# The recurrence's step of a two-layer decoder trunk, with the gate's matmuls set at other places between the groups of small products

## The chip, the cores and the metric

The kernel runs on one core of a Trainium2 chip. The metric is device time in microseconds of one execution, the median of several runs. The core has five engines with a queue each: TensorE (PE, matmuls; PEld is its loading of weights), VectorE (DVE), ScalarE (ACT), GpSimd (POOL) and SyncE (SP), which here only issues DMAs.

## The reference

Two layers over 1024 tokens of width 1024, in float32. The first (gated spatial mixing beside dilated attention) isn't touched. The second is RWKV-7 time mixing: for each of 16 heads of 64 channels a state of 64 x 64 is carried from token to token, and a SiLU gate is multiplied in before the last projection.

```python
def step(state, inp):
    r_t, w_t, k_t, v_t, kk_t, a_t = inp
    sa = jnp.einsum('bhvk,bhk->bhv', state, -kk_t)
    state = (state * w_t[:, :, None, :]
             + sa[..., None] * (kk_t * a_t)[:, :, None, :]
             + v_t[..., None] * k_t[:, :, None, :])
    y_t = jnp.einsum('bhvk,bhk->bhv', state, r_t)
    return state, y_t
...
y = (y + bonus.reshape(B, S, D)).astype(h.dtype) * jax.nn.silu(g)    # g = xg @ w_g
return y @ w_o
```

## The kernel before, in words

The recurrence is computed in 16 chunks of 64 tokens, two chunks to a pair. Within a chunk the token-by-token update is written as products of 64 x 64 blocks, one for each head, and the inverse of a triangular matrix of each head; from chunk to chunk the state S is carried. A product of 64 x 64 uses a quarter of TensorE's array, and a head's products stand in groups: 16 heads, each float32 product as two matmuls, so 32 matmuls and as many weight loads a group (64 where two groups are interleaved).

The matmuls of the gate (x @ w_g, in three float32r products for each block of weights) are independent of the recurrence. They are cut into 128 pieces of three matmuls of 128 x 128 by 128 x 512, and `g1`, `g2` in an order put one or two such pieces at that place. A block of weights for it is loaded (`gl`) and split into a high and a low part (`gx`: a copy on ScalarE, then a subtraction on VectorE, lines 105 and 106).

The order of all engines' work in this part is written out by hand, as strings of names: SCAN_START, then SCAN_STEP six times, then SCAN_END. Each name is a method; each engine executes its own instructions in the order in which the names issue them, so a name's place sets its place on each engine it uses, and on SP's queue for its DMAs. Semaphores are put in from the data's dependences. In a step (chunks c, c+1, with work ahead for c+2 to c+5) the names are:

- `U` (lines 1241 to 1254): products of the inverse X with Ws, interleaved on TensorE with `Wkeys` of the next chunk (line 1225), then two copies to UV on ScalarE.
- `st` (1268 to 1277): products of UV with the transposed keys, then VectorE adds them to the state S; `keep` (1266): GpSimd multiplies S by the decay for the chunk after.
- `Y` and `W` (1285, 1235, 1294): the output's products; those of the state with A, of the next chunk, interleaved with the output's second part; then copies of Ws and Y on ScalarE. W needs the addition of `st`, and the next U needs Ws.
- `al` (1043 to 1048): two groups of products of A with BK, to M and AK through ScalarE's copies; `mA` masks AK on GpSimd. `sM` (1055) stores M, `lM` (1099) loads it again in another layout as Nt.
- `sc` (1030, 1031): the scores' products of A and BK and their copy to MY; `mY` (1084) masks MY of an earlier pair on GpSimd.
- `dec` (1062): GpSimd multiplies BK by the decay in place; `T` (1072, 1073): TensorE transposes the decayed BK.
- `ip`, `ia`, `ie`, `ib` (1106 to 1164): the inversion on VectorE from Nt, of which `ib2`, `ib3` are two and three of the eight parts of its rows; `ic` (1171) stores the inverse (XT<-xm), `lX` (1179) loads it as X. `mx`, `ma`, `mb` (1185, 1197, 1200, 1210, 1213) complete X on VectorE, TensorE and ScalarE.
- `ld`, `uv`, `Yd`, `gl`: loads of A and BK, of v, the store of Y, the load of the gate's weights, all on SP.

TensorE's order in a step is therefore U0 al0 st0 al1 Y0 W1 sc0 U1 sc1 g st1 Y1 g W2 sc2 T0 g sc3 ma0 g2 mb0 g2 T1 g2; SP's is uv1 sM0 ld6 ic0 lM0 lX0 uv2 Yd0 ld7 gl2.

Of the kernel before, what the change touches and what calls it, by code (L numbers as in the profile page):

```python
# [56 lines left out]
SCAN_STEP = (  # L57
    "U0 al0 ib2 st0 al1 Y0 uv1 keep1 mA0 mA1 W1 sM0 sc0 ib3 ld6 U1 sc1 g1 mY0 mY1 ic0 st1 dec0 lM0 Y1 g1 W2 keep2 "
    "ip0 lX0 gx1 uv2 sc2 Yd0 T0 g1 sc3 ia0 ld7 mx0 ma0 dec1 ie0 g2 mb0 g2 T1 g2 ib3 gl2")
SCAN_END = (  # L60
# [1504 lines left out]
```

## Time and profile before

| | |
|---|---|
| median of 3 runs | 1482.53 us (1478.01 to 1484.24) |
| the profiled execution's own time | 1480.0 us |
| span of its instructions | 1478.1 us |
| mean granted clock of TensorE | 0.941 |
| busy: PE / PEld / DVE / ACT / POOL | 1308.3 / 1108.9 / 897.8 / 627.8 / 548.4 us |

The span goes from the first to the last instruction. A busy TensorE isn't one at its peak: matmuls overlap and their ends are modelled. The granted clock is the share of 2.4 GHz that the throttle let through; it has two levels, 1.2 and 2.4 GHz, so 0.941 is a mean over both. The six steps of the recurrence lie between 1089 and 1293 us of the span, the end after them.

### The profile page before, as it was taken

The page shows a single profiled execution, that of the slowest core. Times are in us where ns is not written, and L with a number is a line of the kernel's source. Part 1 is how long each engine was busy: PE and PEld are TensorE (multiplying, and loading weights), DVE is VectorE, ACT ScalarE, POOL GpSimd, SP SyncE. Part 2 cuts the span into 40 slices and gives each one's busy share as a digit, 9 for nine tenths or more (in the row PEclk, how much of TensorE's full clock was granted, in tenths as well). Part 3 has the DMA queues.
Part 4 walks back from the last instruction along what each step waited for, and adds up shares of the span by engine and source line. Part 5 has one row for each costly group of instructions (what it writes and reads, how often), then busy time and mean ns, then how long its engine had stood idle before and what let it go on. Part 6 is the DMA issues. An engine that isn't in the chain of part 4 may idle for free.

```text
span 1478.1 us, 30910 instructions
## 1 busy us (share of the span) xinstructions
PE 1308.3 (89%) x12773; PEld 1108.9 (75%) x12773; DVE 897.8 (61%) x1489; ACT 627.8 (42%) x1188; POOL 548.4 (37%) x353
## 2 busy tenths in 40 slices
PE   5899999899997999999997868998978788887877
PEld 5887788778896799978864436896767666667877
DVE  8741535663557426771599888512856677768884
ACT  4421535552454323552545554323434344454322
POOL 8750102030112612221343353203644444387751
PEclk9999999899999999999999979998978898979998
DMA  6377435350443334224177547517586666676412
GB/s 221 86 259 196 114 128 158 83 131 15 137 121 101 124 119 143 74 74 140 43 220 203 125 103 204 143 48 207 142 244 162 154 168 167 187 212 228 143 36 93
DMA packets 253275, 209.15 MB, mean 141 GB/s; under 512 B 79648, under 2 KB 215424, under 8 KB 253136
## 3 DMA queue, kind: packets, MB, share of 16 engines
q1 hardware_dynamic: 249536, 198.27, 47.1%
q10 hardware_dynamic: 3600, 8.91, 1.8%
q8 instruction: 100, 1.64, 0.5%
q14 instruction: 39, 0.32, 0.1%
HBM read 135.71 MB, written 71.43 MB: 140 GB/s over the span
## 4 chain that ended last, share of the span: by engine, by line
PE 53%; DVE 17%; DMA 9%; issue 8%; ACT 6%; POOL 4%; SPq 2%; ACTq 0%; DVEq 0%; POOLq 0%
PE pj L153 33%; PE pj L943 4%; PE pt L572 2%; PE pj L1477 2%; DMA kl<-dk 1%; DMA BK<-BK_d 1%; DMA w<-in_rw_a_dram 1%; DMA XT<-xm 1%; PE sp L562 1%; PE sp L559 1%; PE op L580 1%; DMA X<-XT 1%; ACT wh L105 1%; PE py L1285 1%; DVE xm L737 1%
## 5 line engine op out<-in xcount | busy, mean ns | idle before, releaser
L106 POOL TENSOR_TENSOR wl<-wraw,wh 128x1024 fp32r<-128x1024 f32 x38 | 93.6, 2466 | 168.6 <-ACT wh L105 157.5
L106 DVE TENSOR_TENSOR wl<-wraw,wh 128x1024 fp32r<-128x1024 f32 x46 | 70.8, 1545 | 94.5 <-ACT wh L105 51.4
L153 PE MATMUL pj<-hh,wh 128*128 128x512 f32 x320 | 127.3, 398 | 0.0
L153 PE MATMUL pj<-hh,wl 128*128 128x512 f32 x320 | 126.6, 396 | 0.0
L153 PE MATMUL pj<-hl,wh 128*128 128x512 f32 x320 | 126.6, 396 | 0.0
L105 ACT ACTIVATE wh<-wraw 128x1024 fp32r<-128x1024 f32 x84 | 88.1, 1056 | 61.9 <-DMA wraw<-in_w_in_even_dram 25.1
L153 PE MATMUL pj<-xl,wh 128*128 128x512 f32 x256 | 102.3, 400 | 2.6 <-DVE xl L740 2.6
L153 PE MATMUL pj<-xh,wh 128*128 128x512 f32 x256 | 102.2, 401 | 2.4 <-ACT ks L789 2.4
L153 PE MATMUL pj<-xh,wl 128*128 128x512 f32 x256 | 101.8, 398 | 0.2 <-POOL wl L106 0.2
L566 DVE CUSTOM_DVE_ANT_0 sc<-sp,tb 128x128 f32<-128x128 f32 (+3 forms) x64 | 48.2, 753 | 59.4 <-PE sp L562 50.8
L1477 PE MATMUL pj<-wh,yh 128*128 128x256 f32 x256 | 75.4, 294 | 5.1 <-DVE x L1481 3.9
L1477 PE MATMUL pj<-wh,yl 128*128 128x256 f32 x256 | 74.4, 291 | 4.6 <-POOL yl L106 4.5
L153 PE MATMUL pj<-wh,hh 128*128 128x256 f32 x256 | 75.1, 296 | 3.2 <-ACT hh L265 2.9
L737 DVE SCALAR_TENSOR_TENSOR xm<-hT,pr,xm 128x512 f32<-128x512 f32 x56 | 50.0, 933 | 44.0 <-ACT xm L736 43.7
L153 PE MATMUL pj<-wh,hl 128*128 128x256 f32 x256 | 75.3, 295 | 1.2 <-DVE hl L266 1.2
L153 PE MATMUL pj<-wh,yl 128*128 128x256 f32 x256 | 73.7, 288 | 1.9 <-POOL yl L624 1.9
L153 PE MATMUL pj<-wl,hh 128*128 128x256 f32 x256 | 74.6, 292 | 0.0
L153 PE MATMUL pj<-wh,yh 128*128 128x256 f32 x256 | 73.3, 286 | 0.8 <-ACT yh L623 0.8
L1477 PE MATMUL pj<-wl,yh 128*128 128x256 f32 x256 | 74.0, 289 | 0.0
L153 PE MATMUL pj<-wl,yh 128*128 128x256 f32 x256 | 72.9, 285 | 0.0
L153 PE MATMUL pj<-wh,xh 128*128 128x256 f32 x256 | 72.2, 282 | 0.6 <-ACT ks L789 0.5
L153 PE MATMUL pj<-wl,xh 128*128 128x256 f32 x256 | 72.2, 282 | 0.0
(320 smaller groups left out, 4062.3 us busy)
## 6 DMA issues: line engine op xcount, KB each, us to landing
wraw<-in_w_in_even_dram SPq DMA_DIRECT2D x28, 512.0 KB
tb<-tb SPq DMA_DIRECT2D x16, 512.0 KB
A_d<-AR SPq DMA_DIRECT2D x16, 512.0 KB
wraw<-in_rw_wg_dram SPq DMA_DIRECT2D x16, 512.0 KB
A<-A_d SPq DMA_DIRECT2D x16, 512.0 KB
BK<-BK_d SPq DMA_DIRECT2D x16, 512.0 KB
xt<-in_x_dram SPq DMA_DIRECT2D x8, 512.0 KB
dv<-vt SPq DMA_DIRECT2D x16, 256.0 KB
```

Source lines behind the costliest of these rows:

```text
L105: nc.scalar.activation(hi, raw, AF.Copy)
L106: sub.tensor_tensor(lo, raw, hi.bitcast(F32), OP.subtract)
L153: nc.tensor.matmul(ps, a(k), b(k), start=(n == 0), stop=(n == 3 * KT - 1))
L559: nc.tensor.matmul(sp[:, c0:c1], qs[:, b * P:(b + 1) * P], kh[:, c0:c1], start=True, stop=False)
L562: nc.tensor.matmul(sp[:, c0:c1], qs[:, b * P:(b + 1) * P], kl[:, c0:c1], start=False, stop=True)
L566: nc.vector.tensor_tensor_reduce(sc[:, :n], sp[:, :n], tb[:, off:off + n], 1.0, BIG, OP.add, OP.min, mn)
L572: nc.tensor.transpose(pt[:, j - j0, :], sc[:, j * P:(j + 1) * P], g.ident)
L580: nc.tensor.matmul(op[:, s0:QW], vt[:, j, :], pth[j // 4][:, j % 4, s0:QW], start=(j == 0), stop=False)
L737: nc.vector.scalar_tensor_tensor(t, hT[kk, f][:, j, 0:512], g.pr[:, i, k:k + 1], t, op0=OP.mult, op1=OP.add)
L943: nc.tensor.matmul(ps, u[:, k], v[:, k % 2], start=(k == 0 and i == 0), stop=(k == KT - 1 and i == 2))
L1285: nc.tensor.matmul(self.py[64 - 64 * e:128 - 64 * e, q], t["MY"][:, 8 * e + q], t["UV"][:, e, q], start=q == 0, stop=False)
L1477: nc.tensor.matmul(ps[:, i, :], u[:, k], v[:, k % 4], start=(k == 0 and j == 0), stop=(k == KT - 1 and j == 2))
```

## The change

The string of the step is written anew; no name is added or left out (the pieces of the gate are nine in both). On TensorE the order becomes U0 al0 g st0 Y0 g W1 al1 U1 g g st1 Y1 sc0 g W2 sc1 T0 g sc2 sc3 ma0 g2 mb0 T1 g. So al1 goes behind W1 (and with it its two copies, mA1 and sM0's data), sc0 behind Y1, sc1 behind W2, T0 ahead of sc2, T1 ahead of the last piece, and the gate's pieces to other places. gx1 goes from behind lX0 to behind U1, so its copy on ScalarE and its subtraction on VectorE stand ahead of st1's addition. dec0 goes behind sc1. SP's order stays as it was.

```diff
 SCAN_STEP = (
-    "U0 al0 ib2 st0 al1 Y0 uv1 keep1 mA0 mA1 W1 sM0 sc0 ib3 ld6 U1 sc1 g1 mY0 mY1 ic0 st1 dec0 lM0 Y1 g1 W2 keep2 "
-    "ip0 lX0 gx1 uv2 sc2 Yd0 T0 g1 sc3 ia0 ld7 mx0 ma0 dec1 ie0 g2 mb0 g2 T1 g2 ib3 gl2")
+    "U0 al0 g1 ib2 st0 Y0 uv1 keep1 g1 W1 al1 mA0 mA1 sM0 ib3 ld6 U1 g1 gx1 g1 mY0 mY1 ic0 st1 lM0 Y1 sc0 g1 W2 "
+    "sc1 dec0 keep2 ip0 lX0 uv2 T0 Yd0 g1 sc2 sc3 ia0 ld7 mx0 ma0 dec1 ie0 g2 mb0 T1 g1 ib3 gl2")
```

## Rows read from the trace of the kernel before

**Rows 1.** Busy time by stretch, a step each, the last the end.
```profile
core 0: us, PE busy (x) PEld busy (x) DVE busy (x) ACT busy (x) POOL busy (x), PEclk, DMA share, GB/s
1089.00:1127.40 38.40, 32.50 (x814) 27.37 (x813) 28.14 (x49) 15.41 (x27) 16.00 (x15) 0.78 0.73 206
...
1160.60:1192.50 31.90, 26.92 (x816) 22.84 (x815) 19.66 (x35) 15.27 (x26) 15.86 (x15) 0.95 0.60 150
...
1292.70:1478.00 185.30, 145.81 (x1671) 136.74 (x1670) 134.95 (x175) 69.58 (x146) 114.80 (x51) 0.88 0.43 143
```

**Rows 2.** Waits of PE, 1089 to 1293 us: total us, times, longest.
```profile
PE pt L1197 <- DMA X<-XT: 10.4, 7, 3.3
PE pm L1030 <- issue: 6.7, 5, 2.7
...
PE pt L1072 <- POOL BK L1062: 2.5, 3, 1.8
```

**Rows 3.** Chain that ended last, 1088 to 1293 us: start us, us, what.
```profile
1152.32 2.86 PE pj L943 x6
...
1163.03 1.15 PE ch L1275 x32
...
1166.11 1.08 PE py L1285 x32
...
1175.37 0.89 PE pj L943 x3
...
1177.57 2.67 issue
...
1184.69 1.29 PE pt L1197 x64
1185.98 1.59 PE pj L943 x6
```

**Rows 4.** DMA queues by packets and MB: 1172.4 to 1177.6, then 1177.6 to 1180.2 us.
```profile
DMA packets 1270, 1.17 MB, mean 226 GB/s; under 512 B 1014, under 2 KB 1014, under 8 KB 1270
q1 hardware_dynamic: 1270, 1.17, 81.2%
...
q1 hardware_dynamic: 1256, 0.45, 84.3%
q8 instruction: 1, 0.02, 2.3%
```

**Rows 5.** Busy time of PE alone, U0 with keys and al0, second step.
```profile
1127.40:1129.50 2.10, 2.10 (x129) 1.00 0.33 125
```

**Rows 6.** Timeline of DVE: start us, us, what, idle before and its releaser.
```profile
1096.76 0.68 DVE L1277 TENSOR_TENSOR S<-ch,S 128x512 f32<-128x512 f32 x1
...
1131.01 0.69 DVE L1277 TENSOR_TENSOR S<-ch,S 128x512 f32<-128x512 f32 x1 [2.99 <-PE ch L1275]
...
1164.22 0.69 DVE L1277 TENSOR_TENSOR S<-ch,S 128x512 f32<-128x512 f32 x1 [1.87 <-PE ch L1275]
...
1179.50 1.23 DVE L106 TENSOR_TENSOR wl<-wraw,wh 128x1024 fp32r<-128x1024 f32 x1 [4.27 <-ACT wh L105]
1182.37 0.42 DVE L1121 TENSOR_TENSOR DN<-Nt,rn 128x256 f32<-128x256 f32 x1 [1.64 <-DMA Nt<-MA]
...
1197.30 0.68 DVE L1277 TENSOR_TENSOR S<-ch,S 128x512 f32<-128x512 f32 x1
...
1263.90 0.69 DVE L1277 TENSOR_TENSOR S<-ch,S 128x512 f32<-128x512 f32 x1 [2.09 <-PE ch L1275]
...
1296.41 0.69 DVE L1277 TENSOR_TENSOR S<-ch,S 128x512 f32<-128x512 f32 x1 [1.33 <-PE ch L1275]
```

**Rows 7.** Timeline of SP, third step: uv1, sM0, lM0, lX0.
```profile
1167.26 1.36 SPq L1013 DMA_DIRECT2D UV<-v_d  x2
1168.72 2.17 SPq L1055 DMA_DIRECT2D MA<-M  x4
...
1174.71 4.43 SPq L1099 DMA_DIRECT2D Nt<-MA  x2
1180.75 2.50 SPq L1179 DMA_DIRECT2D X<-XT  x4
```

**Rows 8.** Timelines of ACT and POOL, third step: the copy of M, dec0.
```profile
1166.06 0.60 ACT L1047 ACTIVATE M<-pt 128x512 f32<-128x512 f32 x1 [1.98 <-PE pt L1043]
...
1175.41 1.91 POOL L1062 TENSOR_TENSOR BK<-BK,EC 128x1024 f32<-128x1024 f32 x1
```

## The prediction

> **What bounds the kernel now.** I first read the busy time by stretch, cut at each start of U0 on TensorE. The change touches the order of six steps of 32 to 38 us; what stands ahead of 1089 us and the end's own order stay as they are [rows 1]. TensorE does the same 814 to 816 matmuls in a step and is busy for 26.9 of 31.9 us in the third, so it waits 5 us; in the first its granted clock was 0.78, in the third 0.95.
>
> Then who TensorE waits for, over the six steps [rows 2]. Three things: the data of `X` for ma0 (10.4 us), the decayed `BK` for T0 (2.5 us), and "issue", a wait for nothing that the profile shows; its largest row is the 6.7 us ahead of the scores. The longest of these, 2.67 us [rows 3], begins at 1177.57. The transfers tell what it is: in the 5.2 us before it no packet moved on the instruction queue, in the 2.6 us of the wait one of 0.02 MB did [rows 4]. TensorE had run through its instructions and waited for the next block. U0 with the keys, then al0, are 129 matmuls in 2.10 us at full clock [rows 5], each with its weight load: instructions leave fastest in the groups of small products, while a gate's piece is 3 matmuls in 0.89 us [rows 3].
>
> So it looks as if TensorE's order were the bound. The third look says otherwise: VectorE's additions to the state (S), one early in each step [rows 6]. From the end of one to the end of the next: 34.3 us, then 132.9 us for the next four loops (33.2 each), then 32.5 us. The addition at 1197.30 has no idle time before it, though TensorE's st0 was waiting for nobody: VectorE was still inverting. So there is a loop beside TensorE's. For the loop from 1164.91 to 1197.98: 3.81 us until sM0's stores start on SP [rows 7], 5.99 us until the loads of `Nt` [rows 7], 7.66 us until VectorE gets it (ia0) [rows 6], 14.93 us of inversion to the next addition, 0.68 us for that: 33.07 us. Work that TensorE saves pays only if this loop shortens too.
>
> **The change part by part.** No instruction is added or removed; the sum is of moves.
>
> *Three gate's pieces leave the tail* (what follows ma0): a double and half of a double, 1.59 + 0.70 = 2.29 us at full clock [rows 3]. They go between al0 and st0, Y0 and W1, U1 and st1. In groups of the gate the step had 3 single and 3 double (7.44 us), it gets 5 and 2 (7.63 us): 0.2 us more.
>
> *al1 moves from before Y0 to after W1.* Its `M` is what sM0 stores. Now M can be copied only after W1 and al1, 128 matmuls, 2.1 us [rows 5], plus the copies of Ws and Y before it and its own 0.60 us [rows 8]: 2.95 us after the addition if TensorE stands ready at W1. That is 0.86 us less than the 3.81 us of now, where uv1's loads, behind Y0, held SP until 1168.62 [rows 7]; Y0 now comes before W1 and uv1 is out of the way. Queued behind sM0 on SP are ld6, ic0, lM0 and lX0, in the same order as before, and who waits for those is ia0, mx0 and ma0. So VectorE's loop becomes 33.07 - 0.86 = 32.2 us. mA1, also later, delays POOL's masks by about a microsecond, and with them dec0, for which see T0.
>
> *TensorE's own loop.* U0 and al0 2.1, a piece 0.89, st0 1.15, Y0 1.08, a piece 0.89, W1 and al1 2.1 [rows 3, 5], M's copy 0.6: sM0 starts 8.8 us after U0. From sM0 to ma0 it was 16.0 us (1168.72 to 1184.69) [rows 3, 7]. From ma0 to the next U0 it was 7.8 us (to 1192.5) [rows 1, 3], now 2.29 us less: 5.5 us. Sum 30.3 us at full clock. In a step that has waited long for X the same two pieces took 2.86 instead of 1.59 us [rows 3]; with 2.5 us for the whole tail at such a clock (1.27 for this double, as much for the products around it) the loop is 32.8 us.
>
> *sc0 and sc1 move behind Y1 and W2, and T0 ahead of sc2.* dec0 multiplies in place what sc1 reads, so it starts only after sc1, which now stands right before T0: TensorE waits there for all of dec0, 1.91 us [rows 8], in every step (2.5 us in all six before [rows 2]). By the durations above T0 starts some 18 us after U0, and T0, a piece and two groups of scores reach ma0 by about 22 us, while X is there at 8.8 + 16.0 = 24.8 us. The wait is hidden by X, with 3 us to spare; without that cover it would be 2 us a step. Behind it on TensorE are T0, sc2 and sc3 only. T1 moves ahead of the last piece; its dec1 has long run.
>
> *The gate's split (gx1) moves ahead of st1's addition.* 1.23 us on VectorE [rows 6] ahead of the second addition, after ScalarE's copy. Covered by Y1, sc0 and a piece on TensorE (1.08 + 0.5 + 0.89 us; the scores are half of al0's number) between st1 and W2: nothing. If the cover is gone, W2 is up to 1.2 us late, and W2 sits before T0, in the shadow of X again. In the old place it stood in VectorE's idle time ahead of ia0 [rows 6].
>
> *The issue waits.* The groups between pieces were U0 to sc1 in one run of nine; now there are pieces after two groups, after two, after three (W1, al1, U1). Bounds: all of the issue waits of a step gone (TensorE at its 30.3 us), or none. Because VectorE's loop of 32.2 us lies above 30.3 us, this term is worth nothing beyond that; it matters only if it makes M late.
>
> The Trainium skill (Runtime: NRT & Kernel Launch, Instruction fetch mechanics) says that crossing a block is mostly hidden, and that TensorE's buffer holds 2048 instructions. By that a step's 1630 would fit and such waits would not be, nor the second rival below, whose chance would go to the forecast; the rows of the wait speak against it.
>
> **The sum.** Both loops lie between 30.3 and 32.8 us; I take 32.0, near VectorE's 32.2. First loop: VectorE stood idle 2.99 us before the addition, waiting for TensorE [rows 6], whose tail shrinks by more than that at the low clock: 3.0 us. Middle four: 33.2 - 32.0 = 1.2 us each, 4.8 us. The last: 0.86 us and the 1.33 us of idle time before its addition [rows 6]: 2.2 us. Together 10.0 us. The end is set by VectorE and GpSimd (135 and 115 of 185 us) [rows 1], which go on from that addition, so I pass the gain on whole. Against the profiled execution (span 1478.1, its time 1480.0 us) that gives 1470.0; that execution lies 2.5 us under the median of 1482.5, so **1472.5 us**. 0.5%, about what a measurement can tell from no change, is 7.4 us: above 1475.1 it counts as the same.
>
> **Rivals.**
> *The forecast, chance 0.50*, 1472.5, own range 1466 to 1478.
> *It gains more, 0.10.* The issue waits go, the clock stays up and VectorE gets Nt earlier than now: loops of 30.3 us. 3.0 + 4 x 2.9 + 3 = 18 us: 1464. For it: the third step's clock of 0.95. Against: X's wait remains.
> *Instructions still run out, now at W1, al1 and U1, 0.30.* These are 192 matmuls in 3.15 us without a piece, more than the 129 in 2.1 us. A wait of 1.2 us there puts M, sM0 and both loops back: 33.2 us again in the middle; first and last loop still give 3.0 + 2.2: 1477.3, no change that can be told.
> *Slower: the late store of M with a low clock, 0.10.* The same shortage by 2.2 us puts sM0 at 11.0 us, X at 27.0 us; TensorE, idle for T0 and then for X, drops to 1.2 GHz, and all of the tail costs as its pieces did (2.86 for 1.59): 9.9 us for 5.5. Loop 8.8 + 2.2 + 16.0 + 9.9 = 36.9 us: 3.7 us more than now, five times, less the 3.0 us of the first: 15.5 us, 1498. It decides when sM0 starts later than 10 us after U0 and the granted clock falls under 0.8. For it: the first step, at 0.78, took 38.4 us [rows 1]. Against: that step also starts late on VectorE.
>
> **The numbers.** Faster: the greater part of the forecast (0.44) and the second case, 0.54. Same: the rest of the forecast and the third, 0.36. Slower 0.10. The range goes past the third case by its uncertainty and takes in the second; the slower one and the far end of the second are left out: 1463 to 1485.
>
> **What would show it.** In the profile after: TensorE's largest wait is for X, 2 us or more in each step; T0 waits about 2 us for `BK` six times (12 us); the issue waits fall well under their half. sM0 starts about 3 us after each addition, additions are 32 us apart, and the one at 1296.41 comes at about 1286. I am wrong if the additions stay 33.2 us apart, or if issue waits stand ahead of al1 and U1. If additions come 30 us apart, it was TensorE's order that bound the kernel.

## The result, and the profile after

The changed kernel is slower. Before: 1476.94 us (median of 15 executions, 1470.29 to 1484.24); after: 1486.77 us (15, 1481.71 to 1494.05); ratio 1.0069, interval 1.0047 to 1.0090. In a later comparison beside other runs it was 1.0076 (1.0047 to 1.0106). I had forecast a gain of 10 us; it is a loss of 10. (The forecast started from 1482.53, the median of the three executions known then; over 15 the kernel before is 5.6 us faster.)

The profiled execution took 1493.6 us with a span of 1491.8, 6.8 us over the median, so its excess over the profile of before is larger than that of the medians. By stretch, again cut at each start of U0, the first, second, fourth and sixth steps and the end (the same view as [rows 1]):

```profile
core 0: us, PE busy (x) PEld busy (x) DVE busy (x) ACT busy (x) POOL busy (x), PEclk, DMA share, GB/s
1084.60:1118.20 33.60, 26.44 (x816) 21.55 (x815) 24.86 (x43) 15.88 (x27) 16.61 (x15) 0.95 0.80 225
1118.20:1157.00 38.80, 29.74 (x812) 24.07 (x811) 29.80 (x45) 15.15 (x26) 16.69 (x15) 0.85 0.60 156
...
1193.30:1229.80 36.50, 30.81 (x812) 24.83 (x811) 23.94 (x41) 15.06 (x27) 16.23 (x15) 0.77 0.56 147
...
1264.60:1306.60 42.00, 31.08 (x805) 24.91 (x804) 21.26 (x39) 13.80 (x24) 13.61 (x14) 0.76 0.67 178
1306.60:1491.80 185.20, 139.51 (x1671) 130.85 (x1670) 133.79 (x176) 69.98 (x147) 114.72 (x51) 0.91 0.40 133
```

The end takes 185.2 us, before 185.3 [rows 1]: nothing was lost there. The six steps take 222.0 us, 203.7 before. Only the first gained (33.6 against 38.4); the others are 34.8 to 42.0 us long, the sixth the longest, and the granted clock is 0.76 to 0.88 in them. The changed kernel's profile in the later comparison took 1486.4 us, close to the median. Its six steps, and the sixth alone:

```profile
1084.20:1299.30 215.10, 174.25 (x4859) 141.94 (x4858) 142.90 (x240) 90.16 (x155) 95.64 (x89) 0.84 0.65 174
...
1257.10:1299.30 42.20, 31.98 (x804) 25.44 (x803) 22.10 (x40) 14.19 (x24) 13.60 (x14) 0.74 0.66 178
```

Steps two to five take 33.9 to 34.8 us there. So the sixth step is long in both profiles; how long the second to fifth are differs from one execution to the next.

Who TensorE waits for in the six steps of the first profile (total us, times, longest; the same view as [rows 2]):

```profile
PE pt L1072 <- POOL BK L1062: 13.9, 6, 3.1
PE pm L1030 <- ACT MY L1031: 10.6, 7, 4.6
PE pj L943 <- ACT wh L105: 6.2, 1, 6.2
PE pt L1210 <- issue: 3.0, 1, 3.0
PE py L1285 <- issue: 2.6, 1, 2.6
...
PE pt L1072 <- ACT X L1213: 2.1, 5, 0.7
```

The wait for X, 10.4 us before, is gone. T0's wait for the decayed `BK` stands in every step, 13.9 us together. New are 10.6 us for the copy of the scores to MY and 6.2 us, once, for the high part of the gate's weights (wh). Both of these copies are ScalarE's. So the next question is what ScalarE waited for, in the same six steps:

```profile
ACT Ws L1238 <- DMA Nt<-MA: 6.3, 1, 6.3
...
ACT wh L105 <- DMA XT<-xm: 4.2, 1, 4.2
ACT MY L1031 <- DMA X<-XT: 4.0, 1, 4.0
ACT MY L1031 <- DMA A<-A_d: 2.2, 1, 2.2
```

None of these pairs makes sense as a dependence: the copy of Ws out of PSUM reads nothing that the load of `Nt` writes. In the profile before there is one such row in the six steps:

```profile
ACT MY L1031 <- DMA Y<-Y: 3.0, 1, 3.0
```

ScalarE's timeline in the changed kernel's fourth step shows what stands between (start us, us, what, idle before and its releaser):

```profile
1208.14 0.60 ACT L949 ACTIVATE XT<-pj 128x512 f32<-128x512 f32 x1 [0.20 <-PE pj L943]
1214.63 0.33 ACTq L950 DMA_DIRECT2D sg_d<-XT  x1
1215.00 0.60 ACT L1238 ACTIVATE Ws<-ch 128x512 f32<-128x512 f32 x1 [6.26 <-DMA Nt<-MA]
1215.49 0.59 ACT L1298 ACTIVATE Y<-py 128x512 f32<-128x512 f32 x1
1215.97 0.60 ACT L1031 ACTIVATE MY<-pm 128x512 f32<-128x512 f32 x1
```

L949 and L950 are the last act of a gate's block: after its eighth piece ScalarE applies SiLU and issues the store of the result (sg_d). SiLU ends at 1208.74; the store is issued at 1214.63, 5.89 us later, and only then do the copies behind it run. Its data was ready. What it waited for is a semaphore: in this step the store signals semaphore 104 when it lands, and so does SP's load of `Nt`, issued at 1208.97. The store's issue waits until that load has landed. The wait is an instruction of the program: an EVENT_SEMAPHORE of line 950 on semaphore 104, which ended at 1214.59, 0.04 us after the load's last update at 1214.55. Line 950 has seven such instructions from 1085 to 1330 us:

```profile
L950 ACTq EVENT_SEMAPHORE  x7: 17/17/17, 1114.5 to 1312.5; - x7
```

So among the semaphore waits that were put in there are some that no dependence of data asks for. The chain that ended last goes through the place:

```profile
1208.97 5.58 DMA Nt<-MA
1214.63 0.33 ACTq L950
1215.00 0.60 ACT Ws L1238
1215.60 0.49 ACT Y L1298
1216.09 0.50 ACT MY L1031
1216.63 1.18 PE pm L1030 x32
```

It is the same in the third step (3.54 us from the end of SiLU to the store, semaphore 109 shared with a load of X), the fifth (1.82 us, 108, a load of A) and the sixth (3.80 us, 108, XT<-xm): 15.1 us in all. In the order before, the eighth piece fell into the tail during the first five steps, and the store went out 0.03 us after its SiLU; only in the sixth was it held, by 2.58 us:

```profile
1280.34 0.64 ACT L949 ACTIVATE XT<-pj 128x512 f32<-128x512 f32 x1
1283.56 0.35 ACTq L950 DMA_DIRECT2D sg_d<-XT  x1
1283.95 0.60 ACT L1031 ACTIVATE MY<-pm 128x512 f32<-128x512 f32 x1 [2.97 <-DMA Y<-Y]
```

I call this the store's hold.

In the sixth step of the changed kernel the held copy is wh, which the next piece of the gate needs at once:

```profile
1275.00 0.60 ACT L949 ACTIVATE XT<-pj 128x512 f32<-128x512 f32 x1
1279.40 0.33 ACTq L950 DMA_DIRECT2D sg_d<-XT  x1
1279.83 1.06 ACT L105 ACTIVATE wh<-wraw 128x1024 fp32r<-128x1024 f32 x1 [4.23 <-DMA XT<-xm]
```

TensorE stood 6.2 us before that piece. Behind it come st1, Y1, sc0, W2 and sc1, and behind sc1 POOL's dec0, which started 10.9 us after the masks; behind dec0 on POOL's queue is ip0, the blank blocks of the inversion. So VectorE waited as well (its waits in the six steps):

```profile
DVE DN L1121 <- DMA Nt<-MA: 36.6, 5, 8.8
DVE S L1277 <- PE ch L1275: 16.6, 6, 4.4
DVE wl L106 <- ACT wh L105: 10.6, 4, 5.7
DVE tm L1131 <- POOL DN L1110: 9.9, 2, 9.1
```

The first row is mostly an exchange: before, VectorE stood 27.4 us ahead of gx1's subtraction (wl), in the same gap, and 6.8 us ahead of `Nt`; now the subtraction runs earlier. The last row is new; 9.1 of its 9.9 us lie in the sixth step. From addition to addition the loops are 31.8, 37.5, 35.6, 36.7, 34.6 and 42 us, against a forecast of 31.3, four of 32.0, and about 30.3. In the later profile they are 32.7, 33.3, 34.2, 33.9, 34.5 and 42.6 us, together 11.6 us more than before, and 10.1 of these are the sixth loop's. There TensorE waited 5.5 us for wh and VectorE 9.0 us for the blank blocks, so these two waits go with the loss that the medians show.

### The profile page after: what moved, and what is told of

The parts are those of the page before. It is cut to its first block, busy times and chain, and to the rows that moved or that the text cites. A ratio compares the mean times of both kernels' runs of the same rounds, so it can differ in the third digit from the quotient of the medians.

```text
span 1491.8 us, 30910 instructions
## 1 busy us (share of the span) xinstructions
PE 1304.8 (87%) x12773; PEld 1102.1 (74%) x12773; DVE 897.9 (60%) x1489; ACT 629.9 (42%) x1188; POOL 549.3 (37%) x353
## 4 chain that ended last, share of the span: by engine, by line
PE 52%; DVE 19%; DMA 9%; issue 7%; ACT 7%; POOL 5%; SPq 2%; ACTq 0%; DVEq 0%; POOLq 0%
PE pj L153 31%; PE pj L943 4%; POOL MY L1084 2%; PE pj L1477 2%; PE pt L572 2%; PE pj L711 1%; DMA Nt<-MA 1%; DVE rt L198 1%; PE sp L559 1%; PE sp L562 1%; ACT wh L105 1%; PE op L580 1%; DVE wl L106 1%; PE pt L1210 1%; DVE rr L201 1%
## 5 line engine op out<-in xcount | busy, mean ns | idle before, releaser
L106 DVE TENSOR_TENSOR wl<-wraw,wh 128x1024 fp32r<-128x1024 f32 x46 | 70.1, 1530 | 81.1 <-ACT wh L105 35.6
```

The lines of the kernel that those rows point to most:

```text
L106: sub.tensor_tensor(lo, raw, hi.bitcast(F32), OP.subtract)
```

## The experiments

There are two theories beside the prediction's own. A: the store's hold makes the loss; what it costs hangs on what stands behind it on ScalarE. B: the loss is in the new order itself, T0 directly behind sc1 and dec0, and the late scores.

**The store later, and T0 behind sc2.** Four runs on one chip. (In the cuts of the orders the strings are broken at the same names, so that the difference stands out.) The edit that sends the store later keeps SiLU where it is and issues the DMA at the step's end (a new name, gs):

```diff
-        g.nc.scalar.dma_start(g.sg_d[n % KT, :, f * 512:(f + 1) * 512], t)
+        self.held.append((g.sg_d[n % KT, :, f * 512:(f + 1) * 512], t))
+        if not self.hold:
+            self.store()
...
+    def store(self):
+        for dst, t in self.held:
+            self.g.nc.scalar.dma_start(dst, t)
+        self.held = []
...
-    "sc1 dec0 keep2 ip0 lX0 uv2 T0 Yd0 g1 sc2 sc3 ia0 ld7 mx0 ma0 dec1 ie0 g2 mb0 T1 g1 ib3 gl2")
+    "sc1 dec0 keep2 ip0 lX0 uv2 T0 Yd0 g1 sc2 sc3 ia0 ld7 mx0 ma0 dec1 ie0 g2 mb0 T1 g1 gs0 ib3 gl2")
```

The first run is the changed order with that edit. Expected:

> The changed order, but in the six steps the store of the gate's result (sg_d) is issued on ScalarE at the end of the step, behind T1 and the last piece, instead of right behind its SiLU. Theory A, the store's issue holds ScalarE: in the changed kernel ScalarE stood 6.3, 4.2, 4.0 and 2.2 us behind it, until an unrelated DMA (Nt, XT, X, A) had landed, and TensorE then waited 4.6 and 2.0 us for MY and 6.2 us for the split weight. Without it these waits go: ScalarE's waits for DMAs near 0, TensorE's for MY from 10.6 to about 5 us, for the weight from 6.2 to about 0: 8 to 12 us faster than the changed kernel, ratio to before 0.999 to 1.002. Theory B, T0 behind dec0 (13.9 us of TensorE's waits) and the pause at sc3 cost it: ratio stays at 1.005 to 1.009. Theory C, the low clock and the instruction blocks by themselves: ratio stays too, with issue waits at 13 us.

The second leaves the store in its place and moves T0:

```diff
-    "sc1 dec0 keep2 ip0 lX0 uv2 T0 Yd0 g1 sc2 sc3 ia0 ld7 mx0 ma0 dec1 ie0 g2 mb0 T1 g1 ib3 gl2")
+    "sc1 dec0 keep2 ip0 lX0 uv2 Yd0 g1 sc2 T0 sc3 ia0 ld7 mx0 ma0 dec1 ie0 g2 mb0 T1 g1 ib3 gl2")
```

> The changed order with one move: T0 goes behind sc2, so that a piece and sc2 stand between sc1 and T0, and T0 between sc2 and sc3. Theory B: TensorE's wait for the decayed BK falls from 13.9 us to 3 to 6 us and the wait of sc3 for the copy of sc2 (0.78 us five times) goes: 8 to 12 us faster than the changed kernel, ratio 0.999 to 1.002. Theory A: the waits move behind ScalarE's hold and the gain is under 5 us, ratio above 1.004.

The third has both edits:

> Both edits: the store at the step's end and T0 behind sc2. If A and B each cost what their waits say, 16 to 22 us faster than the changed kernel: ratio 0.992 to 0.996, the gain that was forecast (0.993). If another bound lies below (VectorE's loop of 32.2 us, or X), the second edit adds less than 4 us to the first: ratio 0.997 to 1.000.

The fourth is the control, the order of before with the late store (gs0 ahead of the tail's ib3):

> The order of before, with the gate's store at the end of the step as in the first run: the control. In the order of before the store held ScalarE once, for 3.0 us in the sixth step. Theory A: at most those 3 us, ratio 0.998 to 1.000. If the late store gains by itself, by any other way, ratio under 0.997.

Measured, as ratios to the kernel before on the same chip (1478.41 us): late store 0.9991 (0.9971 to 1.0012), T0 behind sc2 alone 1.0043 (1.0021 to 1.0065), both 0.9984 (0.9964 to 1.0004), control 0.9974 (0.9953 to 0.9996). In the changed order with the late store ScalarE waits for no transfer in the six steps, and TensorE's waits become:

```profile
PE pt L1080 <- POOL BK L1070: 14.8, 6, 3.2
PE pm L1038 <- ACT MY L1039: 4.7, 6, 0.8
...
PE pj L944 <- ACT wh L105: 1.9, 1, 1.9
```

(Lines are 1 to 10 higher in these kernels.) The wait for MY falls from 10.6 to 4.7 us and that for wh from 6.2 to 1.9; T0's for `BK` stays. The steps:

```profile
1081.00:1281.70 200.70, 163.07 (x4860) 133.70 (x4859) 136.85 (x233) 89.69 (x155) 97.07 (x89) 0.91 0.65 173
```

That is 21.3 us under the 222.0 us of the changed kernel's profile, in which the same 4860 matmuls kept TensorE busy for 176.3 us at a clock of 0.83. So 13 of the 21 us are the same products at a higher clock and 8 are idle time. That is one profile against one, and the clock does not follow from the hold alone: the kernel with T0 moved and the hold left has 163.5 us at 0.92. In both kernels whose store is late the loss is gone, and with T0 moved but the hold left most of it stays. The third theory of the first expectation, the low clock and the instruction blocks by themselves, had the ratio stay; it fell, with issue waits of 12.9 us as in the changed kernel. Theory A holds for the bulk; T0's place is worth some 4 us by 1.0069 against 1.0043, with intervals that overlap, and nothing that can be told with the late store.

With both, TensorE's waits in the six steps are:

```profile
PE pt L1205 <- DMA X<-XT: 8.9, 8, 3.0
PE pt L1080 <- POOL BK L1070: 3.2, 6, 0.9
```

T0's 14.8 us shrank to 3.2, and 8.9 us of wait for X came back: whichever stands first on TensorE takes the time, and the balance is nothing that can be told (0.9984 against 0.9991). The control shows that the order of before gains from the late store too, and that against it the new order gains nothing. Theory A had at most 3 us for the control, 0.998 to 1.000, and 0.9974 lies just under that, with an interval that reaches into it. Nor did the late store free the control of holds: in its sixth step the store met a load of the gate's weights and held the copies to UV.

```profile
1287.46 1.19 ACT L1262 ACTIVATE UV<-ch 64x512 f32<-64x512 f32 x2 [6.38 <-DMA wraw<-in_rw_wg_dram]
```

So the removed hold of 2.6 us does not explain the control's 3.8 us; noise, or another effect of the store's place, isn't excluded.

**One part at a time.** From here on the base is the kernel before, with parts of the change put in; the store is in its place unless the label says late. First the three pieces and gx1 alone:

```diff
-    "U0 al0 ib2 st0 al1 Y0 uv1 keep1 mA0 mA1 W1 sM0 sc0 ib3 ld6 U1 sc1 g1 mY0 mY1 ic0 st1 dec0 lM0 Y1 g1 W2 keep2 "
-    "ip0 lX0 gx1 uv2 sc2 Yd0 T0 g1 sc3 ia0 ld7 mx0 ma0 dec1 ie0 g2 mb0 g2 T1 g2 ib3 gl2")
+    "U0 al0 g1 ib2 st0 al1 Y0 uv1 keep1 mA0 mA1 g1 W1 sM0 sc0 ib3 ld6 U1 sc1 g1 gx1 g1 mY0 mY1 ic0 st1 dec0 lM0 Y1 "
+    "g1 W2 keep2 ip0 lX0 uv2 sc2 Yd0 T0 g1 sc3 ia0 ld7 mx0 ma0 dec1 ie0 g2 mb0 T1 g1 ib3 gl2")
```

> The kernel before with only three gate's pieces and gx1 moved to where the change has them; al1, sc0, sc1, dec0, T0 and sc2 stay where they were before, and the store of the gate's result stays right behind its SiLU. Theory A (the store, which travels with the pieces, holds ScalarE's queue until an unrelated transfer has landed): this part alone loses most of what the change loses, 6 to 12 us against before (ratio 1.004 to 1.008), and ScalarE shows waits on transfers like Nt<-MA and X<-XT of 8 us or more in the six steps. Rival B (the loss came from sc0, sc1 and dec0 standing late, so that ip0 on POOL and with it the inversion stands late): within 0.3% of before (0.997 to 1.003). ScalarE's waits of under 4 us would speak against A whatever the time is.

Then the same with the late store (gs0 as above):

> The run before this one (pieces and gx1 moved alone) with the store of the gate's result issued at the end of the step. Theory A: the loss is gone, ratio to before 0.995 to 1.001, and 5 to 12 us under the run with the store in its place; no ScalarE wait on Nt<-MA, X<-XT or A<-A_d. If pieces between the groups of small products cost TensorE by themselves (longer issue waits, a lower clock), it stays above 1.003. If they are worth what the prediction had for the tail, it is 3 us or more under the 1474.4 us of the control with the old order and the late store.

Then that with al1 moved:

```diff
-    "U0 al0 g1 ib2 st0 al1 Y0 uv1 keep1 mA0 mA1 g1 W1 sM0 sc0 ib3 ld6 U1 sc1 g1 gx1 g1 mY0 mY1 ic0 st1 dec0 lM0 Y1 "
+    "U0 al0 g1 ib2 st0 Y0 uv1 keep1 g1 W1 al1 mA0 mA1 sM0 sc0 ib3 ld6 U1 sc1 g1 gx1 g1 mY0 mY1 ic0 st1 dec0 lM0 Y1 "
```

> The run before this one plus al1 moved to behind W1: all of the change but the late places of sc0, sc1, dec0 and the early one of T0. The prediction's terms for al1 (VectorE's loop 0.86 us shorter per step by stores that start sooner) would give 4 to 6 us less than the run before it; if the loop is not the bound, or the stores do not start sooner, less than 2 us of difference. VectorE's loops from state addition to state addition: 32.2 us by the prediction, 33 if al1 does nothing.

And the changed order with the late store and T0 behind sc2, with ip0 ahead of dec0:

```diff
-    "sc1 dec0 keep2 ip0 lX0 uv2 Yd0 g1 sc2 T0 sc3 ia0 ld7 mx0 ma0 dec1 ie0 g2 mb0 T1 g1 gs0 ib3 gl2")
+    "sc1 ip0 dec0 keep2 lX0 uv2 Yd0 g1 sc2 T0 sc3 ia0 ld7 mx0 ma0 dec1 ie0 g2 mb0 T1 g1 gs0 ib3 gl2")
```

> The run with the late store and T0 behind sc2 (1475.8 us in its comparison), with ip0 ahead of dec0 on POOL, so that the blank blocks of the inversion do not stand behind the decay that waits for sc0. There the sixth loop was 35.0 us, with VectorE 5.6 us in wait for POOL's DN. If that queue costs time, the sixth loop falls to 30 to 32 us and the whole by 2 to 4 us, to 1472 to 1474; if other waits take its place, less than 1 us. It makes 1.0 to 1.2 us of POOL work earlier, so dec0 and T0 may come about 1 us later in every step, and that rival would give no change or 2 us more.

Measured beside 1477.08 us: pieces alone 1.0003 (0.9985 to 1.0021), pieces with the late store 0.9974 (0.9952 to 0.9996), with al1 too 0.9981 (0.9962 to 1.0001), ip0 first 1.0016 (0.9996 to 1.0036).

The first is a miss of theory A in its simple form: the store was held by 9.3 us over the six steps (Nt<-MA, X<-XT and XT<-xm again), and yet the loss is nothing that can be told. The hold by itself is not the price. Taking it away still gave 4 us, so A and B had to be joined (theory C from here on, another than the first expectation's): a hold costs what the work queued behind it is worth. In the changed order that is sc0 and sc1, with dec0, T0 and ip0 behind them; in this run those were done. al1, to which I had given more than half of the gain, is worth 0.9981 against 0.9974: nothing. With ip0 first, the sixth loop did fall from 35.0 to 32.7 us, but dec0 came later in each step and T0's wait rose from 3.2 to 13.8 us, the rival that stood in the expectation.

**Which part goes with the hold.** The run with al1 above, but with the store in its place:

> The kernel before with the three pieces, gx1 and al1 moved, the store in its place behind the SiLU; sc0, sc1, dec0, T0 and sc2 where they were. The pieces alone held ScalarE by 9.1 us over the step's SiLUs and still came out at 1.0003. Theory C (the hold costs most where the masked scores stand behind it: in the changed order the copies of sc0 and sc1 queue behind the store, with dec0, ip0 and T0 behind them): without the late scores this run stays within 0.3% of before, 0.998 to 1.003. Rival D (it is al1, whose M would be copied behind the held store so that sM0 starts late): 1.004 or more.

The pieces and gx1 with the late scores:

```diff
-    "U0 al0 g1 ib2 st0 al1 Y0 uv1 keep1 mA0 mA1 g1 W1 sM0 sc0 ib3 ld6 U1 sc1 g1 gx1 g1 mY0 mY1 ic0 st1 dec0 lM0 Y1 "
-    "g1 W2 keep2 ip0 lX0 uv2 sc2 Yd0 T0 g1 sc3 ia0 ld7 mx0 ma0 dec1 ie0 g2 mb0 T1 g1 ib3 gl2")
+    "U0 al0 g1 ib2 st0 al1 Y0 uv1 keep1 mA0 mA1 g1 W1 sM0 ib3 ld6 U1 g1 gx1 g1 mY0 mY1 ic0 st1 lM0 Y1 sc0 "
+    "g1 W2 sc1 dec0 keep2 ip0 lX0 uv2 sc2 Yd0 T0 g1 sc3 ia0 ld7 mx0 ma0 dec1 ie0 g2 mb0 T1 g1 ib3 gl2")
```

> The kernel before with the three pieces, gx1 and sc0, sc1, dec0 moved, the store in its place; al1, T0 and sc2 where they were. Theory C: this pair makes most of the loss, ratio 1.003 to 1.008, with waits of VectorE on POOL's DN or of TensorE on POOL's BK of over 10 us together. Rival D: within 0.3% of before.

The changed kernel again, without an edit:

> The changed kernel itself, unaltered, beside the two parts on the same chip: 1.005 to 1.009 to before, as in its own comparison (1.0069). If it comes out within 0.3% of before, part of what was measured as the change's loss belongs to that comparison, and the sums over its parts are to be read by this run.

And the late scores alone, sc0, sc1 and dec0 moved in the same way in the string of before:

> The kernel before with only sc0, sc1 and dec0 at the change's late places; pieces, gx1, al1, T0, sc2 and the store where they were. Theory C wants a hold ahead of the late scores, and here the gate's block ends in the tail as before: within 0.3% of before. If the late scores cost by themselves (dec0 late, POOL's blank blocks late, a longer wait of T0), 1.003 or more, and theory C is then only half of it.

Measured beside 1476.39 us: pieces and al1 1.0015 (0.9992 to 1.0038), pieces and scores 1.0057 (1.0031 to 1.0082), the change again 1.0076, scores alone 1.0030 (1.0012 to 1.0048). The pair of pieces and late scores makes most of the loss, as C has it, with VectorE's wait for POOL's blank blocks the largest of all runs:

```profile
DVE tm L1131 <- POOL DN L1110: 16.9, 6, 9.6
```

The late scores alone were to cost nothing and cost 4 us. Their trace shows why that run was no clean one. The sixth step, in which before has its one hold, had a longer one:

```profile
1280.64 0.60 ACT L949 ACTIVATE XT<-pj 128x512 f32<-128x512 f32 x1
1290.18 0.39 ACTq L950 DMA_DIRECT2D sg_d<-XT  x1
1290.61 0.60 ACT L1031 ACTIVATE MY<-pm 128x512 f32<-128x512 f32 x1 [9.38 <-DMA bor<-bo_d]
```

The store shared its semaphore (106) with a load that the end asks for; 8.95 us went by, and TensorE waited 7.8 us for the copy of rt behind it. Which transfer the store meets changes with the order, and with it the price.

**The late scores without the hold, and the store on another queue.** The last two orders with the late store (gs0 as above): first the late scores alone,

> The kernel before with only sc0, sc1 and dec0 at the change's late places, and the store of the gate's result at the step's end. Without the late store this order was 1.0030 to before; its sixth step then showed a hold of 8.95 us, on a load that the end has asked for (bor<-bo_d). If that hold was its whole loss, this comes out as the control with the old order and the late store did, 0.996 to 0.999. If the late scores cost by themselves (dec0 late, T0 and POOL's blank blocks behind it), it stays at 1.001 or more.

then pieces, gx1 and late scores,

> The kernel before with the pieces, gx1, sc0, sc1 and dec0 at the change's places, and the late store; without it this was 1.0057. Hold as the whole cause: 0.996 to 1.000, and VectorE's wait for POOL's DN, 16.9 us there, falls under 6 us. If the pieces between the groups together with the late scores cost TensorE or POOL by themselves: 1.003 or more.

and the changed kernel with one word altered:

```diff
-        g.nc.scalar.dma_start(g.sg_d[n % KT, :, f * 512:(f + 1) * 512], t)
+        g.nc.gpsimd.dma_start(g.sg_d[n % KT, :, f * 512:(f + 1) * 512], t)
```

> The changed kernel in its own order, with one word altered: the store of the gate's result, still right behind its SiLU, is issued on POOL's queue instead of ScalarE's. If the loss is that ScalarE's queue is held, ScalarE has no wait on transfers left and the time falls by 6 to 12 us from the 1487 of the changed kernel, to a ratio of 0.998 to 1.003. POOL may now be held instead, with dec0 and ip0 behind the store: then ScalarE's waits are gone too, but the ratio stays at 1.004 or more and VectorE and TensorE wait for POOL's DN and BK for more than the 9.9 and 13.9 us of the changed kernel.

Measured beside 1477.77 us: scores late, store late 0.9984 (0.9966 to 1.0002); pieces and scores with the late store 1.0015 (0.9996 to 1.0033); store on POOL 1.0049 (1.0027 to 1.0072). The first says that the late scores cost nothing by themselves, though its store too met a load for the end (bor) and held ScalarE 3.8 us behind the sixth step. The second lost its hold and 6 us, but VectorE still waits 14.5 us for POOL's blank blocks, where I expected under 6, so some 2 to 6 us of the late scores together with the pieces may be real; the full change with the late store, which has them too, is at 0.9991, so this is left open. The third took the hold off ScalarE, whose waits for transfers are gone, and put another in its place, on POOL:

```profile
POOL sg_d L950 <- ACT XT L949: 15.3, 4, 9.4
```

The store has semaphores of its own there (111 to 118) and meets no foreign transfer, but POOL executes in order too, and now its queue stands until SiLU is done. T0's wait for `BK` is 16.7 us (13.9 in the changed kernel), VectorE's for the blank blocks 9.0 (9.9), and from the end's addition to the last instruction it takes 184.4 us where the others take 180 to 182. So the second case of the expectation came: the hold of ScalarE is gone and most of the loss stays. How the 1.0049 divides between POOL's queue in the steps and the end isn't separated.

**All pairs side by side.** Hold: from the end of SiLU to the issue of the store, summed over the profile's six steps. Price: the difference of the two ratios times 1477 us. Sixth loop: from VectorE's addition in the sixth step to the next step's, in place and late, one profile each (of the change also the later one).

| order | store in place | store late | hold, us | price, us | sixth loop, us |
|---|---|---|---|---|---|
| before | 1 | 0.9974 | 2.6 | 3.8 | 32.5, 32.3 |
| pieces, gx1 | 1.0003 | 0.9974 | 9.3 | 4.3 | 34.3, 34.1 |
| pieces, gx1, al1 | 1.0015 | 0.9981 | 12.2 | 5.0 | 34.8, 35.9 |
| late scores | 1.0030 | 0.9984 | 9.0 | 6.8 | 37.4, 30.5 |
| pieces, gx1, late scores | 1.0057 | 1.0015 | 10.1 | 6.2 | 40.4, 38.7 |
| the change, T0 behind sc2 | 1.0043 | 0.9984 | 15.3 | 8.7 | 40.7, 35.0 |
| the change | 1.0069 | 0.9991 | 15.1 | 11.5 | 42.0 and 42.6, 34.7 |

A ratio is uncertain by about 0.002, so a single price by some 4 us; but all seven have one sign, and the largest two belong to the largest holds. In four rows the two ratios come from different comparisons, in at least three of these from two chips, and a late store is not always one without a hold (above). The orders that lose with the store in its place have a long sixth loop, 37 us and more; the first two rows with pieces have none, and in their sixth step the hold was 0.2 and 0.4 us. No run changed that one hold alone, so whether it or the late scores behind the store make the price isn't separated. In the row of pieces and late scores the sixth loop stays long with the late store too. In the column of the late store the change and its parts lie between 0.9974 and 1.0015, before's own order at the lower end. The two whose intervals lie below 1 are the old order and the pieces with gx1, each with the late store: 1474.4 and 1474.8 us.

## Why the prediction was wrong

**The step that failed** is the first of the parts, "0.2 us more" for the gate's pieces. I costed their matmuls and not what a piece carries: each eighth one ends a block, and its SiLU and the issue of its store go with it to the new place, onto ScalarE's queue. In the tail that store found its semaphore free in five steps of six; in the middle of the step it meets SP's bursts, and is held by 1.8 to 5.9 us in four steps. Measured, the store in its new place costs the changed order 11.5 us against the late store (1.0069 against 0.9991), as much as the loss of 10 us; the order of before gains 3.8 us by the same late store, so some 8 of the 11.5 are the new order's own. The part by itself came out even: pieces and gx1 alone are at 1.0003, with holds of 9.3 us. The loss came where the late scores, with dec0 and the blank blocks behind them, and in the sixth step wh stood behind the store; I had priced these parts one by one. The row that would have warned me stood in the profile before: ScalarE's MY behind the store of Y, 3.0 us in the sixth step, a pair with no dependence.

**The forecast gain of 10 us did not come either.** With the hold out of the way the change stands at 0.9991, the old order with the same late store at 0.9974; the medians are 1474.7 and 1474.4 us. By its terms:

- *al1 later, stores of M earlier, 0.86 us a loop*: sM0 started 3.3 to 4.4 us after the addition, 3.8 on average, not 2.95. The 3.81 us of before was one step's; all six are 2.5 to 3.9, 3.4 on average, so there was less to gain than I summed, and the stores start later now. My condition, "if TensorE stands ready at W1", didn't hold; SP, freed of uv1, waited for the copy of M, 13.0 us over the six steps. Pieces with al1 against pieces without gave 0.9981 against 0.9974: no gain.
- *T0's wait is hidden by X, with 3 us to spare*: wrong. The wait is there as forecast, 2.1 to 3.1 us six times, 13.9 us for my 12. But ma0 came 24.6 to 27.9 us after U0 in five steps and 34.7 in the sixth, and not 22, later than X, so there was no shadow: X's wait vanished and T0's took its place. My sum to ma0 had left out the directly following waits, sc3 for sc2's copy (0.8 us a step) and the issue waits, and a clock of 0.76 to 0.88 in five of the steps.
- *Issue waits well under their half*: not shown. By all rows they are 14.6 us before and 12.9 after, but 7.5 in the later profile of the same kernel, so one profile each can't tell what the pieces between the groups are worth. They stand elsewhere (2.99 us in the midst of mb0's products in the second step, 2.57 us amid the output's products in the first). The Trainium skill (Runtime: NRT & Kernel Launch, Instruction fetch mechanics) calls the crossing of a block mostly hidden, and the profiles agree with that: 38 packets of 16 KB moved on the instruction queue in the six steps, before and after, and one of them fell into a wait of 2 us or more before (2.67 us), two after (2.99 and 2.57). The shorter issue waits after, 1.3 to 1.8 us, have no such packet beside them, so instruction blocks explain only a part of this term.
- *gx1 costs nothing*: nearly right where there was no hold, 1.9 us once with the late store; in the sixth step its copy stood behind the store, and TensorE waited 6.2 us.
- *The first loop gains 3.0 us*: 31.8 us where I had 31.3, and the step 33.6 against 38.4: right in that profile; the later one has 32.7 and 35.4.
- *The end passes the time on whole*: right; from the addition of the end to the last instruction it takes 181.0 us before and 180 to 182 us in the profiles of the changed kernel and of its orders with the late store.

**The rival on the slow side** (0.10, 1498) had the sign, and the changed kernel's steps did run at a lower clock, 0.83 and 0.84 in its two profiles against 0.89; that the idle time lowered it isn't shown, for two orders with the hold and the loss ran at 0.92 and 0.93. Its cause was another: I had M late by missing instructions, and sM0 was not late by that. The range, 1463 to 1485, ended 2 us below the result, and was so near only because its base was too high: from 1476.9 us the same forecast would have missed by 20 us and the same range by 7.

What stays open: whether the late scores with the pieces cost a few us of their own, how much of the price belongs to the sixth step's hold alone, why the control gained, and how the semaphores of the transfers are dealt out. I did not try to give the store on ScalarE a semaphore of its own.

## What to carry to other kernels

Cost a moved step by everything it issues, down to what happens once in eight times, and look at each queue for what then stands behind a DMA's issue: a store that waits holds the whole queue of the engine that issues it. A row in the waits whose two ends share no data ("Ws behind the load of Nt") is the sign of such a hold; it can be looked for in the profile before, and was there. Issue a store that nobody needs soon at a place where the engine has nothing urgent behind it, here the step's end, before tuning the order of anything else, and look again for holds there: in the control the store met another load at that place too.

## What the runs showed of the hardware that I had not expected

- A DMA's issue on ScalarE waited for a transfer of SP's with the same completion semaphore: with `Nt` (104) 5.89 us, with a load of X (109) 3.54, with a load for the end (106) 8.95. The transfers' data had nothing to do with each other; the wait is an EVENT_SEMAPHORE instruction in the program, and all that stood behind it on ScalarE's queue waited too.
- The same matmuls of the six steps kept TensorE busy for 176.3 us at a mean clock of 0.83 and for 163.1 at 0.91. What lowered the clock isn't shown.
- Two groups of scores in direct succession cost TensorE 0.8 us of wait for the first one's copy, in each step, also with the late store (4.7 us in six).
- The sum of TensorE's issue waits in the six steps differs between two executions of one kernel as much as between the orders: 12.9 and 7.5 us after, 14.6 before.
